# A hybrid encoder layer on one core: a third buffer for keys and values, and decays exponentiated a head ahead without the key norm

## The chip, the cores and the metric

The kernel runs on one core of one Trainium2 chip. The metric is device time in microseconds (us): the median over several executions, each timed on the device. Engines are named as the profile names them: PE (TensorE), DVE (VectorE), ACT (ScalarE), POOL (GpSimd), SP (SyncE).

## The reference

One encoder layer over 1024 tokens of width 1024, all in float32. After an RMSNorm one projection feeds two branches; only branch A (a gated delta rule in both directions, 8 heads of width 128) is touched by the change. Of it, per head and direction:

```python
    q = to_chunks(q * (dk ** -0.5))          # q, k l2-normalised per token
    g = jnp.cumsum(to_chunks(g), axis=-1)    # log decays
    diff = g[..., :, None] - g[..., None, :]
    decay = jnp.where(incl, jnp.exp(jnp.where(incl, diff, 0.0)), 0.0)
    kb = k * beta[..., None]
    lower = jnp.where(strict, jnp.einsum("bhnid,bhnjd->bhnij", kb, k) * decay, 0.0)
    rhs = jnp.concatenate([v * beta[..., None], kb * jnp.exp(g)[..., None]], axis=-1)
    sol = lax.linalg.triangular_solve(lower, rhs, left_side=True, lower=True,
                                      unit_diagonal=True)
    ...
    attn = jnp.einsum("bhnid,bhnjd->bhnij", q, k) * decay
    def step(S, inp):
        v_new = u_n - jnp.einsum("bhcd,bhde->bhce", w_n, S)
        o = (jnp.einsum("bhcd,bhde->bhce", qd_n, S)
             + jnp.einsum("bhij,bhje->bhie", attn_n, v_new))
        S = S * jnp.exp(gl_n)[..., None, None] + jnp.einsum("bhcd,bhce->bhde", kd_n, v_new)
```

q, k and v come from the projection through a centred convolution over 5 tokens and a SiLU. Branch B is a gated linear attention with 4 heads. Both are gated, projected, merged, projected once more and added to x.

## The kernel before

Tokens are cut into 8 chunks of 128 (NT), so a head has 16 units (U): 8 chunks in each direction. Branch A goes head by head, with four functions for each:

- `gdn_project(h)` multiplies the normalised input by the head's columns for q, k, v and z (four projections of 48 products of 128x128x512 each, tiles `pj_a` and `pj_z`), copies q, k and v into padded tiles `xp` and convolves them on VectorE by one multiplication (L516) and four multiply-adds (L518), in the order k, q, v. The SiLU (L499) of q, k, v and of the head before's z (`zs`) follows on ScalarE, between two loads of ScalarE's function tables: SiLU is in one table set, Exp and Ln in another.
- `gdn_decay(h)` fetches the head's cumulated log decays, spread over all partitions (1 MB, L580), into the tile `dt` and fills the half that must vanish with -1e30 by two selects on POOL (L585). There are two `dt` buffers; `dt` becomes the attention matrix later (L743) and is read to the end of the scan.
- `gdn_inverse(h)` builds the triangular inverse of all 16 units at once. The keys are transposed (`pk`), copied (`ktok`, L601) and squared with a sum (L605) into n2; rk2 = 1/n2. The Ln of n2 (L613) goes into a bias, and sixteen Exp (L622) make the decay times 1/n2 out of `dt`. Four products of VectorE (L633) multiply it with keys times keys (`pgr`) into `um`. Then come a small inverse of 32x32 blocks by 120 VectorE operations `tmp` and `yl` (L655, L657), products p, py, px, p2, p3 on TensorE that put blocks together, v times the key norm (L734) and `dt` times keys-queries (L743).
- `gdn_scan(h)` steps through the chunks in both directions: products `psc` (L781, L786, L796), r (L783), vd (L789), a copy vn on ScalarE (L791), the state S (L801), outputs `po` (L770); at its end o, osq and zs are combined and the head is written out.

What runs when is decided ahead of time: a scheduler lists the instructions of each engine in one fixed order, by the priorities that the blocks of the last loop set (a lower number goes first), by dependences and by free buffers. The inverse of head h+1 runs beside the scan of head h, and projections of the next heads, which have the last priority (P_FILL), fill TensorE in between; after head 7 thirteen gate projections (`pj_t`) do so, then branch B and the last projections follow. A tile asked for under a tag with n buffers waits until the tile n requests ago is no longer read: q, k and v (tags a0, a1, a2) have two buffers each, `xp` three. v's buffer is also `vtok`, which the scan reads to its end.

Of the kernel before, what the change touches and what calls it, by code (L numbers as in the profile page):

```python
# [8 lines left out]
F32 = mybir.dt.float32  # L9
F32R = mybir.dt.float32r  # L10
AF = mybir.ActivationFunctionType
ALU = mybir.AluOpType

P = 128
# [18 lines left out]

WRAW, WSPLIT, XS, XP = 2, 4, 4, 3

# [53 lines left out]
def layer_kernel(  # L89
# [43 lines left out]
    def by128(t):  # L133
        return t.rearrange("p (n i) -> p n i", i=P)
# [266 lines left out]
    def scan_gates(pool):  # L401
# [8 lines left out]
        smT = pool.tile([64, T], F32, tag="osq", name="smT", bufs=1)  # L410
        stl = pool.tile([P, 2, P], F32, tag="stl", name="stl", bufs=1)
        nc.scalar.dma_start(stl, consts[:, CONSTS["su"][0]:CONSTS["su"][0] + 2 * P].rearrange("p (d i) -> p d i", d=2))
        mid = pool.tile([P, 2, 130], F32, tag="t2", name="mid", bufs=4)
        nc.scalar.dma_start(mid, consts[:, o_c:o_c + 260].rearrange("p (d i) -> p d i", d=2))
        strict = [stl[:, d] for d in range(2)]
        ones = part(tb_, 3, 1)
# [30 lines left out]
        for d in range(2):  # L447
            rhs = lg[:, d].rearrange("p h n -> p (h n)")
            for q, m in enumerate((mask[d], strict[d], ones)):
                o = (d * 3 + q) * 64  # L450
                nc.tensor.matmul(psg[:, o:o + 64], lhsT=m, rhs=rhs, start=True, stop=True)

            o = 384 + d * 64
            nc.tensor.matmul(psg[:, o:o + 64], lhsT=mid[:, d, :P], rhs=rhs, start=True, stop=True)
        nc.scalar.activation(ev, psg[:, :384].rearrange("p (d q h n) -> p d q h n", d=2, q=3, h=HA), AF.Exp)
# [41 lines left out]
    def gdn_project(h, pool):  # L497
        a = [pool.tile([P, T], F32, tag=f"a{j}", name=f"{'qkv'[j]}{h}", bufs=2) for j in range(3)]
        silu = lambda t: tc.keep_in_program_order(nc.scalar.activation(t, t, AF.Silu))  # L499
# [76 lines left out]
    def gdn_decay(h, pool):  # L576


        dt = pool.tile([P, U, P], F32, tag="dt", name=f"dt{h}", bufs=2)
        nc.sync.dma_start(dt.rearrange("p u i -> p (u i)"),  # L580
                          cr_d[h:h + 1].rearrange("h d t -> h (d t)").broadcast_to([P, 2 * T]))
        for d in range(2):
            s = 1 - 2 * d
            us = slice(d * NT, (d + 1) * NT)
            nc.gpsimd.affine_select(dt[:, us], dt[:, us], pattern=[[0, NT], [s, P]], compare_op=ALU.is_ge,  # L585
                                    fill=-1e30, base=0, channel_multiplier=-s)
        return dt

    def gdn_inverse(h, pool, sm, qkv, dt):
# [21 lines left out]
        c2 = sm.tile([P, 2, NT], F32, tag="c2", name=f"c2_{h}")  # L611

        tc.keep_in_program_order(nc.scalar.activation(nk, n2, AF.Ln))  # L613
        bias = sm.tile([P, 2, NT], F32, tag="bias", name=f"bias_{h}")
        nc.vector.tensor_tensor(bias, nb[:, :, h], nk.unsqueeze(1).broadcast_to([P, 2, NT]), op=ALU.subtract)
        nc.vector.tensor_tensor(c1, be[:, :, h], rk2.unsqueeze(1).broadcast_to([P, 2, NT]), op=ALU.mult)
        nc.vector.tensor_tensor(c2, c1, ev[:, :, 1, h], op=ALU.mult)
        for g in range(2):
            for d in range(2):
                for n in range(4 * g, 4 * g + 4):  # L620
                    u = d * NT + n
                    nc.scalar.activation(dt[:, u], dt[:, u], AF.Exp, bias=bias[:, d, n:n + 1])  # L622


        um = pool.tile([P, U, P], F32, tag="um", name=f"um{h}", bufs=2)
        for g in range(2):
            pk = bank(pg, "g", f"pgr{h}_{g}")
            for j in range(4):
                ns = slice((4 * g + j) * P, (4 * g + j + 1) * P)
                nc.tensor.matmul(pk[:, j * P:(j + 1) * P], lhsT=kT[:, ns], rhs=kT[:, ns], start=True, stop=True)  # L630
            for d in range(2):
                us = slice(d * NT + 4 * g, d * NT + 4 * g + 4)
                nc.vector.tensor_tensor(um[:, us], by128(pk), dt[:, us], op=ALU.mult)  # L633

# [91 lines left out]

        tc.keep_in_program_order(nc.scalar.activation(nk, nk, AF.Exp, scale=0.5))

# [7 lines left out]
        for g in range(2):  # L736
# [4 lines left out]
            for d in range(2):  # L741
                us = slice(d * NT + 4 * g, d * NT + 4 * g + 4)
                nc.vector.tensor_tensor(dt[:, us], by128(pk), dt[:, us], op=ALU.mult)  # L743
        return dt, um, ktok, vtok, c2

    def gdn_scan(h, pool, sm, qkv, dt, um, ktok, vtok, c2):
        qT, kT, _ = qkv
# [24 lines left out]
        for s in range(NT):  # L772
# [12 lines left out]
            for d, n in un:  # L785
                nc.tensor.matmul(pc[d][:, P:2 * P], lhsT=um[:, d * NT + n], rhs=r[d], start=True, stop=True)  # L786
                if s < NT - 1:
                    vd[d] = sm.tile([P, P], F32, tag=f"vd{d}", name=f"vd{h}_{d}_{s}", bufs=1)
                    nc.vector.tensor_scalar(vd[d], pc[d][:, P:2 * P], c2[:, d, n:n + 1], None, op0=ALU.mult)  # L789
                vn[d] = sm.tile([P, P], F32, tag=f"vn{d}", name=f"vn{h}_{d}_{s}", bufs=1)  # L790
                nc.scalar.copy(vn[d], pc[d][:, P:2 * P])  # L791
            S0 = list(S)
# [363 lines left out]
```

## Time and profile before

| | |
|---|---|
| time, median of 3 runs | 1640.31 us (1637.06 to 1645.77) |
| the profiled execution | 1647.96 us, span of the trace 1646.2 us |
| TensorE busy | 1538.3 us, 93% |
| VectorE busy | 871.7 us, 53% |
| ScalarE busy | 704.3 us, 43% |
| GpSimd busy | 190.5 us, 12% |

The first two rows are device times; the profiled execution lies 7.65 us above the median and 1.76 us above its own span. Busy times are shares of the span. Branch A takes the first 870 us or so.

### The profile page before, as it was taken

What the parts mean: (1) busy time and instruction counts of PE and PEld (TensorE: products, weight loads), DVE (VectorE), ACT (ScalarE), POOL (GpSimd) and SP (SyncE); (2) the same over time, 40 slices, a digit from 0 to 9 for tenths busy, and PEclk for the clock granted to TensorE, in tenths of its full rate; (3) what the DMA queues carried; (4) which work ended last, traced back from release to release, by engine and by line L of the source; (5) the groups of instructions that cost most, each with busy time, mean ns of one, the idle gap of its engine ahead of it and who ended that gap; (6) DMA issues with size and microseconds to landing.
All of it is one profiled execution on the core that took longest, in us unless ns stands there. A gap on an engine that the chain in (4) does not pass through costs nothing.

```text
span 1646.2 us, 24982 instructions
## 1 busy us (share of the span) xinstructions
PE 1538.3 (93%) x9500; PEld 1295.8 (79%) x9500; DVE 871.7 (53%) x2252; ACT 704.3 (43%) x1488; POOL 190.5 (12%) x207
## 2 busy tenths in 40 slices
PE   6988978998998999899899999999999999999998
PEld 6867866777787878787677888898898988787887
DVE  5485485877879696878531012323314336445413
ACT  5452454436363635554332233535425545423311
POOL 3220111111213011110000020010120100000000
PEclk9996987999898999999999999999999999999999
DMA  5320221131212113131233322131131234755414
GB/s 160 126 68 18 80 71 33 33 106 36 96 46 90 46 33 116 50 99 48 77 121 100 103 65 64 27 103 33 55 85 48 80 100 143 238 157 173 128 45 154
DMA packets 142435, 142.07 MB, mean 86 GB/s; under 512 B 11419, under 2 KB 115403, under 8 KB 141285
## 3 DMA queue, kind: packets, MB, share of 16 engines
q1 hardware_dynamic: 134546, 126.11, 25.6%
q10 hardware_dynamic: 7128, 12.26, 2.4%
q0 software_dynamic: 640, 2.10, 0.4%
q8 instruction: 75, 1.23, 0.3%
q14 instruction: 46, 0.38, 0.1%
HBM read 109.98 MB, written 30.46 MB: 85 GB/s over the span
## 4 chain that ended last, share of the span: by engine, by line
PE 64%; DVE 16%; ACT 11%; DMA 5%; issue 3%; SPq 0%; POOL 0%; ACTq 0%; DVEq 0%; POOLq 0%
PE pj_t L252 8%; PE pj_y L252 7%; PE pj_v L241 6%; PE pout L141 5%; PE pj_g L252 5%; DVE yl L657 4%; PE pj_a L252 4%; DVE tmp L655 4%; PE pj_z L252 4%; PE pj_k L252 3%; PE pj_q L252 2%; ACT dt L622 2%; PE po L770 2%; PE psb L948 2%; PE pob L970 2%
## 5 line engine op out<-in xcount | busy, mean ns | idle before, releaser
L252 PE MATMUL pj_a<-hh,hi_a 128*128 128x512 f32 x368 | 153.6, 417 | 16.5 <-ACT xp L504 9.4
L252 PE MATMUL pj_a<-hl,hi_a 128*128 128x512 f32 x368 | 152.6, 415 | 0.0
L252 PE MATMUL pj_a<-hh,lo_a 128*128 128x512 f32 x368 | 152.1, 413 | 0.0
L252 PE MATMUL pj_t<-hh,hi_t 128*128 128x512 f32 x256 | 103.9, 406 | 2.8 <-ACT gt L282 2.8
L252 PE MATMUL pj_t<-hh,lo_t 128*128 128x512 f32 x256 | 104.2, 407 | 0.0
L252 PE MATMUL pj_t<-hl,hi_t 128*128 128x512 f32 x256 | 103.7, 405 | 0.0
L182 POOL TENSOR_TENSOR lo_a<-raw_a,hi_a 128x512 fp32r<-128x512 f32 x48 | 63.8, 1329 | 311.0 <-ACT hi_a L178 257.0
L252 PEld LDWEIGHTS pj_a<-hh,hi_a 128*128 128x128 f32 x368 | 73.0, 198 | 31.6 <-ACT xp L504 10.2
L657 DVE TENSOR_TENSOR yl<-yl,tmp 128x54 f32<-128x54 f32 (+13 forms) x480 | 96.3, 241 | 0.1
L655 DVE TENSOR_TENSOR tmp<-ulb,yl 128x54 f32<-128x54 f32 (+13 forms) x480 | 90.4, 228 | 0.1
L252 PEld LDWEIGHTS pj_a<-hl,hi_a 128*128 128x128 f32 x368 | 72.4, 197 | 13.9 <-issue 0.7
L252 PEld LDWEIGHTS pj_a<-hh,lo_a 128*128 128x128 f32 x368 | 72.4, 197 | 13.7 <-issue 0.8
L252 PE MATMUL pj_y<-ob,hi_y 128*128 128x512 f32 x256 | 79.1, 390 | 0.9 <-DVE gb L1075 0.9
L141 PE MATMUL pout<-wo,hh 128*128 128x512 f32 (+1 forms) x272 | 79.7, 377 | 0.0
L791 ACT COPY vn<-psc 128x128 f32<-128x128 f32 x128 | 32.2, 265 | 108.5 <-DVE vd L789 72.1
L241 PE MATMUL pj_v<-lo_v,hh 128*128 128x256 f32 x256 | 72.5, 283 | 0.0
L241 PE MATMUL pj_v<-hi_v,hl 128*128 128x256 f32 x256 | 72.5, 283 | 0.0
L241 PE MATMUL pj_v<-hi_v,hh 128*128 128x256 f32 x256 | 72.5, 283 | 0.0
L796 PE MATMUL psc<-vd,ktok 128*128 128x128 f32 x224 | 45.4, 304 | 24.8 <-ACT vn L791 24.7
L182 POOL TENSOR_TENSOR lo_v<-raw_v,hi_v 128x512 fp32r<-128x512 f32 x32 | 41.3, 1290 | 233.1 <-ACT hi_v L178 229.0
L796 PEld LDWEIGHTS psc<-vd,ktok 128*128 128x128 f32 x224 | 34.7, 198 | 39.5 <-ACT vn L791 37.7
L184 DVE TENSOR_TENSOR lo_t<-raw_t,hi_t 128x512 fp32r<-128x512 f32 x32 | 22.0, 689 | 71.7 <-ACT hi_t L178 71.7
(315 smaller groups left out, 4024.2 us busy)
## 6 DMA issues: line engine op xcount, KB each, us to landing
raw_a<-in_w_in_dram SPq DMA_DIRECT2D x48, 256.0 KB
dt<-cr_d SPq DMA_DIRECT2D x8, 1024.0 KB
qe<-eg_d SPq DMA_DIRECT2D x16, 512.0 KB
raw_t<-in_w_in_dram SPq DMA_DIRECT2D x32, 256.0 KB
gt_d<-gt SPq DMA_DIRECT2D x64, 128.0 KB
raw_v<-in_w_in_dram SPq DMA_DIRECT2D x32, 256.0 KB
xt<-in_x_dram SPq DMA_DIRECT2D x8, 512.0 KB
raw_z<-in_w_in_dram SPq DMA_DIRECT2D x16, 256.0 KB
```

The source lines that it names most:

```text
L141: nc.tensor.matmul(ps, lhsT=a(k), rhs=b(k), start=(s == 0), stop=(s == len(steps) - 1))
L182: nc.gpsimd.tensor_tensor(lo, raw, hi.bitcast(F32), op=ALU.subtract)
L241: nc.tensor.matmul(ps[b][:, c * 256:(c + 1) * 256], lhsT=a[th][:, kk, ts], rhs=w[:, k, :], start=kk == 0 and i == 0 and c == 0, stop=kk == ...
L252: nc.tensor.matmul(ps[:, cols], lhsT=a[:, k, :], rhs=b[th][:, kk, cols], start=kk == 0 and a is hi and b is src[0], stop=kk == KD - 1 and ...
L622: nc.scalar.activation(dt[:, u], dt[:, u], AF.Exp, bias=bias[:, d, n:n + 1])
L655: nc.vector.tensor_tensor(tv, ul2[:, i, 0:i].unsqueeze(2).broadcast_to([P, i, w_]), yv[:, i].unsqueeze(1).broadcast_to([P, i, w_]), op=ALU ...
L657: nc.vector.tensor_tensor(yv[:, 0:i], yv[:, 0:i], tv, op=ALU.subtract)
L770: nc.tensor.matmul(po_n(n), lhsT=lhsT, rhs=rhs, start=count[b] == 1, stop=count[b] == len(todo[b]))
L791: nc.scalar.copy(vn[d], pc[d][:, P:2 * P])
L796: nc.tensor.matmul(pc[d][:, 2 * P:3 * P], lhsT=ktok[:, ns], rhs=vd[d], start=True, stop=True)
L948: nc.tensor.matmul(p_s[:, :256], lhsT=ktok[:, u], rhs=vt[:, n], start=True, stop=True)
L970: nc.tensor.matmul(po[e][:, j * P:(j + 1) * P], lhsT=a, rhs=b, start=(i == 0), stop=(i == len(todo) - 1))
```

## The change

`A_BUFS` gives k (a1) and v (a2) three buffers, `xp` loses one, and two constant tiles share one buffer. `gdn_decay` exponentiates `dt` itself, with a bias that no longer holds the key norm. It is called for head h+1 right after the inverse of head h, so the sixteen Exp stand a head ahead of where their values are used. The factor 1/n2 comes back in two places: in `um`, by sixteen operations of 128x128 with rk2 as a scalar per partition, and in vn, by an ACTIVATE with rk2 as its scale. The Ln and Exp that make the key norm for v stand together behind p3.

```diff
-WRAW, WSPLIT, XS, XP = 2, 4, 4, 3
+WRAW, WSPLIT, XS, XP = 2, 4, 4, 2
+
+A_BUFS = (2, 3, 3)
...
-        stl = pool.tile([P, 2, P], F32, tag="stl", name="stl", bufs=1)
...
-        mid = pool.tile([P, 2, 130], F32, tag="t2", name="mid", bufs=4)
...
+        msk = pool.tile([P, 4, P], F32, tag="t2", name="msk", bufs=4)
...
-        a = [pool.tile([P, T], F32, tag=f"a{j}", name=f"{'qkv'[j]}{h}", bufs=2) for j in range(3)]
+        a = [pool.tile([P, T], F32, tag=f"a{j}", name=f"{'qkv'[j]}{h}", bufs=A_BUFS[j]) for j in range(3)]
...
             nc.gpsimd.affine_select(dt[:, us], dt[:, us], pattern=[[0, NT], [s, P]], compare_op=ALU.is_ge,
                                     fill=-1e30, base=0, channel_multiplier=-s)
+            for n in range(NT):
+                nc.scalar.activation(dt[:, d * NT + n], dt[:, d * NT + n], AF.Exp, bias=nb[:, d, h, n:n + 1])
         return dt
...
-
-        tc.keep_in_program_order(nc.scalar.activation(nk, n2, AF.Ln))
-        bias = sm.tile([P, 2, NT], F32, tag="bias", name=f"bias_{h}")
-        nc.vector.tensor_tensor(bias, nb[:, :, h], nk.unsqueeze(1).broadcast_to([P, 2, NT]), op=ALU.subtract)
...
-        for g in range(2):
-            for d in range(2):
-                for n in range(4 * g, 4 * g + 4):
-                    u = d * NT + n
-                    nc.scalar.activation(dt[:, u], dt[:, u], AF.Exp, bias=bias[:, d, n:n + 1])
...
-            for d in range(2):
-                us = slice(d * NT + 4 * g, d * NT + 4 * g + 4)
-                nc.vector.tensor_tensor(um[:, us], by128(pk), dt[:, us], op=ALU.mult)
+            for j in range(4):
+                n = 4 * g + j
+                for d in range(2):
+                    u = d * NT + n
+                    nc.vector.scalar_tensor_tensor(um[:, u], pk[:, j * P:(j + 1) * P], rk2[:, n:n + 1], dt[:, u],
+                                                   op0=ALU.mult, op1=ALU.mult)
...
-        tc.keep_in_program_order(nc.scalar.activation(nk, nk, AF.Exp, scale=0.5))
+        tc.keep_in_program_order(nc.scalar.activation(nk, n2, AF.Ln))
+        nc.scalar.activation(nk, nk, AF.Exp, scale=0.5)
...
-                nc.scalar.copy(vn[d], pc[d][:, P:2 * P])
+                nc.scalar.mul(vn[d], pc[d][:, P:2 * P], rk2[:, n:n + 1])
```

The scheduler lists every engine's instructions anew. Three places of these lists follow.

ScalarE, the front of head 4 (pk_1_4838 and pk_1_4893 are its keys in PSUM, the last squares; vn_0_3 and the like belong to scan 3, zs to head 3). Before:

```order
L605 ACTIVATE pk_1_4838,n_4_4827<-pk_1_4838 128x128
L791 COPY vn_0_3_4691<-psc_0_3_4680 128x128
L791 COPY vn_1_3_4696<-psc_1_3_4681 128x128
L613 ACT_TABLE_LOAD
L613 ACTIVATE nk_4849<-n_4_4827 128x8
L499 ACT_TABLE_LOAD
L499 ACTIVATE zs_4586<-zs_4586 128x1024
L622 ACT_TABLE_LOAD
L622 ACTIVATE dt_4285<-dt_4285,bias_4855 128x128 x16
L639 COPY ul_4890<-um_4875 32x32x8 x4
```

And in the changed kernel:

```order
L607 ACTIVATE pk_1_4893,n_4_4882<-pk_1_4893 128x128
L788 ACTIVATE vn_1_2_4723<-psc_1_2_4708,rk_3_3915 128x128
L788 ACTIVATE vn_0_3_4746<-psc_0_3_4735,rk_3_3915 128x128
L500 ACTIVATE zs_4641<-zs_4641 128x1024
L311 ACT_TABLE_LOAD
L180 CAST hi_a_5_0_5376<-raw_a_5_0_5374 128x512
L635 COPY ul_4938<-um_4911 32x32x8 x4
```

The Ln, the sixteen Exp and two of three table loads have left the stretch between the last squares and ul, the first copy out of um.

ScalarE behind the end of scan 2 (osq_3667 and osq_4655 belong to the ends of scan 2 and the start of scan 3, dt_4324 is head 4's dt, gz are head 4's z columns, q_4348 and q_4293 its q). Before:

```order
L727 ACTIVATE nk_3871<-nk_3871 128x8
L178 CAST hi_a_5_0_4546<-raw_a_5_0_4544 128x512
L282 COPY gz_0_0_4574<-pj_z_0_4512 128x256
L282 COPY gz_0_1_4577<-pj_z_0_4512 128x256
L791 COPY vn_0_0_4609<-psc_0_0_4604 128x128
L791 COPY vn_1_0_4614<-psc_1_0_4605 128x128
L178 CAST hi_a_5_1_5281<-raw_a_5_1_5279 128x512
...
L309 ACT_TABLE_LOAD
L499 ACTIVATE q_4293<-q_4293 128x1024
```

And in the changed kernel:

```order
L489 ACTIVATE osq_3667<-pm_a_1_3885,eps_eq 128x512
L490 ACTIVATE osq_3667<-osq_3667 128x1024
L788 ACTIVATE vn_0_0_4664<-psc_0_0_4659,rk_3_3915 128x128
L588 ACTIVATE dt_4324<-dt_4324,nb 128x128 x16
L752 ACTIVATE osq_4655<-q_3360 128x1024
L788 ACTIVATE vn_1_0_4669<-psc_1_0_4660,rk_3_3915 128x128
L284 COPY gz_0_0_4629<-pj_z_0_4567 128x256
L284 COPY gz_0_1_4632<-pj_z_0_4567 128x256
...
L311 ACT_TABLE_LOAD
L788 ACTIVATE vn_0_2_4718<-psc_0_2_4707,rk_3_3915 128x128
L500 ACTIVATE q_4348<-q_4348 128x1024
```

Head 4's sixteen Exp now stand between the first two vn of scan 3 and ahead of gz and of the SiLU of head 4.

VectorE, the convolution of head 3's keys (k3; numbers behind a name are heads: um2 and v2 belong to inversion 2, r1 and osq1 to scan 1). Before:

```order
L725 COPY um2_2919<-p3_2_3261 64x8x64
L801 SCALAR_TENSOR_TENSOR S1_1_6_2830<-S1_1_5_2802,ev_532,psc1_1_6_2809 128x128
L783 SCALAR_TENSOR_TENSOR r1_0_7_2839<-psc1_0_7_2836,nE_533,v1_1361 128x128
L734 TENSOR_TENSOR v2_2339<-pv2_0_3281,nk_2_2893 128x512
L734 TENSOR_TENSOR v2_2339<-pv2_1_3287,nk_2_2893 128x512
L783 SCALAR_TENSOR_TENSOR r1_1_7_2842<-psc1_1_7_2837,nE_533,v1_1361 128x128
L516 TENSOR_SCALAR k3_3316<-xp1_3_3318,cw_110 128x1024
L743 TENSOR_TENSOR dt2_2329<-pkq2_0_3293,dt2_2329 128x512 x2
L743 TENSOR_TENSOR dt2_2329<-pkq2_1_3300,dt2_2329 128x512 x2
L817 TENSOR_TENSOR osq1_2644<-osq1_2644,o1_2854 128x512 x2
L518 SCALAR_TENSOR_TENSOR k3_3316<-xp1_3_3318,cw_110,k3_3316 128x1024
```

And in the changed kernel:

```order
L702 COPY um1_1947<-py_1_2226 32x8x32 x2
L703 COPY xa1_2185<-px_1_2259 32x8x32
...
L517 TENSOR_SCALAR k3_3361<-xp1_3_3363,cw_110 128x1024
L519 SCALAR_TENSOR_TENSOR k3_3361<-xp1_3_3363,cw_110,k3_3361 128x1024
L721 COPY um1_1947<-p3_1_2301 64x8x64
...
L731 TENSOR_TENSOR v1_1386<-pv1_0_2322,nk_1_1940 128x512
...
L740 TENSOR_TENSOR dt1_1360<-pkq1_0_2334,dt1_1360 128x512 x2
```

The convolution moved from the end of scan 1 and of inversion 2 to the end of inversion 1, a head earlier. On TensorE the transposes of head 3's keys (pk) stood 95 rows behind the last products of inversion 2 (pkq) and stand 2 rows behind them now.

## Rows read from the trace of the kernel before

**Rows 1.** the page, part 1: busy us, share of the span, instructions

```profile
PE 1538.3 (93%) x9500; PEld 1295.8 (79%) x9500; DVE 871.7 (53%) x2252; ACT 704.3 (43%) x1488; POOL 190.5 (12%) x207
```

**Rows 2.** busy time of each engine in stretches of the span

```profile
core 0: us, PE busy (x) PEld busy (x) DVE busy (x) ACT busy (x) POOL busy (x), PEclk, DMA share, GB/s
...
471.00:560.00 89.00, 82.34 (x593) 68.10 (x592) 69.92 (x211) 43.80 (x98) 19.15 (x18) 0.92 0.22 69
...
870.00:1000.00 130.00, 129.36 (x664) 110.80 (x664) 17.50 (x26) 36.02 (x76) 13.51 (x12) 1.00 0.32 87
sum 915.00, PE 834.74 PEld 697.03 DVE 583.38 ACT 398.72 POOL 123.14; mean PE 92.75 PEld 77.45 DVE 64.82 ACT 44.30 POOL 13.68
```

**Rows 3.** the chain of waits, parts of it in order: start, us, what

```profile
260.93 3.03 PE p L686 x64
...
330.34 1.84 PE p L686 x64
...
377.97 2.25 ACT pk L605 x16
...
432.63 2.52 PE p L686 x64
...
849.58 8.22 PE pj_t L252 x36
```

**Rows 4.** ScalarE in order of time, front of head 4

```profile
473.30 1.28 ACT L613 ACT_TABLE_LOAD   x1
...
474.82 1.28 ACT L499 ACT_TABLE_LOAD   x1
476.11 1.06 ACT L499 ACTIVATE zs<-zs 128x1024 f32<-128x1024 f32 x1
477.18 1.28 ACT L622 ACT_TABLE_LOAD   x1
478.47 4.80 ACT L622 ACTIVATE dt<-dt,bias 128x128 f32<-128x128 f32 x16
```

**Rows 5.** VectorE in order of time, fronts of heads 2 and 4

```profile
290.01 0.17 DVE L608 TENSOR_SCALAR n<-n 128x8 f32<-128x8 f32 x1 [0.95 <-ACT pk L605]
...
295.57 0.69 DVE L633 TENSOR_TENSOR um<-pgr,dt 128x512 f32<-128x512 f32 x1 [0.48 <-ACT dt L622]
...
472.99 0.17 DVE L608 TENSOR_SCALAR n<-n 128x8 f32<-128x8 f32 x1 [0.72 <-ACT pk L605]
...
473.64 0.17 DVE L617 TENSOR_TENSOR c<-c,ev 128x16 f32<-128x16 f32 x1
...
483.30 0.69 DVE L633 TENSOR_TENSOR um<-pgr,dt 128x512 f32<-128x512 f32 x1 [0.48 <-ACT dt L622]
```

**Rows 6.** groups by line: busy us, mean ns, idle before and what ended it

```profile
L622 ACT ACTIVATE dt<-dt,bias 128x128 f32<-128x128 f32 x128 | 38.3, 388 | 0.4 <-DVE bias L615 0.3
L791 ACT COPY vn<-psc 128x128 f32<-128x128 f32 x128 | 32.2, 265 | 108.5 <-DVE vd L789 72.1 <-PE psc L786 17.8 <-DVE tmp L655 12.5
...
L518 DVE SCALAR_TENSOR_TENSOR k<-xp,cw,k 128x1024 f32<-128x1024 f32 x32 | 43.4, 1357 | 0.1
...
L783 DVE SCALAR_TENSOR_TENSOR r<-psc,nE,v 128x128 f32<-128x128 f32 x112 | 36.9, 344 | 13.2 <-PE psc L781 11.2
...
L633 DVE TENSOR_TENSOR um<-pgr,dt 128x512 f32<-128x512 f32 x32 | 22.1, 691 | 27.7 <-ACT dt L622 24.5 <-PE pj_z L252 3.1
```

**Rows 7.** waits of the weight load queue, 284 to 870 us: total, times, longest

```profile
PEld psc L796 <- ACT vn L791: 35.6, 32, 3.8
```

**Rows 8.** fetches and selects of dt, SP and POOL in order of time

```profile
418.80 0.46 SPq L580 DMA_DIRECT2D dt<-cr_d  x1
...
424.69 3.92 POOL L585 TENSOR_SCALAR_AFFINE_SELECT dt<-dt 128x1024 f32<-128x1024 f32 x2 [6.38 <-DMA dt<-cr_d]
...
514.54 0.34 SPq L580 DMA_DIRECT2D dt<-cr_d  x1
...
519.16 5.81 POOL L585 TENSOR_SCALAR_AFFINE_SELECT dt<-dt 128x1024 f32<-128x1024 f32 x2
```

More of the change, by code (lines that the diff above doesn't have):

```diff
@@ L410, in scan_gates @@
         smT = pool.tile([64, T], F32, tag="osq", name="smT", bufs=1)
-        stl = pool.tile([P, 2, P], F32, tag="stl", name="stl", bufs=1)
-        nc.scalar.dma_start(stl, consts[:, CONSTS["su"][0]:CONSTS["su"][0] + 2 * P].rearrange("p (d i) -> p d i", d=2))
-        mid = pool.tile([P, 2, 130], F32, tag="t2", name="mid", bufs=4)
-        nc.scalar.dma_start(mid, consts[:, o_c:o_c + 260].rearrange("p (d i) -> p d i", d=2))
-        strict = [stl[:, d] for d in range(2)]
+        msk = pool.tile([P, 4, P], F32, tag="t2", name="msk", bufs=4)
+        nc.scalar.dma_start(msk[:, 0:2], consts[:, CONSTS["su"][0]:CONSTS["su"][0] + 2 * P].rearrange("p (d i) -> p d i", d=2))
+        nc.scalar.dma_start(msk[:, 2:4], consts[:, o_c:o_c + 260].rearrange("p (d i) -> p d i", d=2)[:, :, :P])
+        strict, mid = ([msk[:, 2 * q + d] for d in range(2)] for q in range(2))
         ones = part(tb_, 3, 1)
@@ L453, in scan_gates @@
             o = 384 + d * 64
-            nc.tensor.matmul(psg[:, o:o + 64], lhsT=mid[:, d, :P], rhs=rhs, start=True, stop=True)
+            nc.tensor.matmul(psg[:, o:o + 64], lhsT=mid[d], rhs=rhs, start=True, stop=True)
         nc.scalar.activation(ev, psg[:, :384].rearrange("p (d q h n) -> p d q h n", d=2, q=3, h=HA), AF.Exp)
@@ L743, in gdn_inverse, with gdn_scan @@
                 nc.vector.tensor_tensor(dt[:, us], by128(pk), dt[:, us], op=ALU.mult)
-        return dt, um, ktok, vtok, c2
-    def gdn_scan(h, pool, sm, qkv, dt, um, ktok, vtok, c2):
+        return dt, um, ktok, vtok, rk2, c2
+    def gdn_scan(h, pool, sm, qkv, dt, um, ktok, vtok, rk2, c2):
         qT, kT, _ = qkv
```

## The prediction

> **What bounds the kernel now.** I read the busy times first. TensorE is busy 93% of the span, VectorE 53%, ScalarE 43% [rows 1]. The table by stage then shows where TensorE is not full: between 85 and 1000 us it is idle for 915.00 - 834.74 = 80.3 us, and from 870 us on, when the gate projections fill it, it is busy 129.36 of 130 us [rows 2]. So whatever the change gives must come out of the eight heads of branch A: the number of products is the same before and after, and the end is their time plus TensorE's idle and slow stretches.
>
> Next I read the chain of waits by its marks, one per head: the first products p of a head's inversion (line 686) [rows 3]. From one mark to the next I cut three parts: the **middle** (p of head h to the last square of head h+1's keys), the **front** (those squares to the last um), and the **inversion** (um to p, almost all of it VectorE, 120 small tmp/yl operations and what the scheduler put between them). Head 4's front stands as it ran on ScalarE [rows 4] and VectorE [rows 5]: a table load for the Ln, a load and the SiLU of zs, another load, then sixteen Exp in 4.80 us; VectorE's four um products wait for them one by one. From 472.99 to 483.30 + 0.69 it is 11.0 us; heads 3 to 7 are all alike. Head 2 has no loads there and takes 290.01 to 296.26, 6.3 us [rows 5]. Head 1, read in the same way, lies at 10.2.
>
> **The change, part by part.**
>
> *The front.* The Ln, the bias and the Exps are gone. What is left is n2, rk2, c1 and c2 (472.99 to 473.64 + 0.17: 0.82 us) [rows 5] and sixteen um operations of 128x128 where there were four of 128x512. No such um is in the trace. The nearest row is r (line 783): the same operation, one PSUM operand, a scalar per partition, 128x128, 344 ns by its mean [rows 6]; two behind each other overlap by some 0.05, and I take 0.30 each: 4.8 us, bounds 0.27 and 0.344, that is 4.3 to 5.5. The new front is 0.8 + 4.8 = 5.6 us. Saved: 5.4 us in each of heads 3 to 7 (4.7 to 5.9 by the bounds), 4.6 in head 1, 0.7 in head 2. Head 0 loses: the Exps of dt(0) and dt(1) come into ScalarE's order ahead of what its front needs; I count twelve Exps of 0.30 us start to start (4.80 / 16 [rows 4]) that nothing hides, +3.4 net of the two loads that go. Sum of the fronts: -27.0 - 4.6 - 0.7 + 3.4 = -28.9 us.
>
> [...]
>
> The split therefore costs VectorE about 4.8 - 2.8 = 2.0 us a head by rows, which is inside the 5.4 above.
>
> *The loads.* In the orders ScalarE has 57 table loads before and 42 after. Each takes 1.28 us, and the next ACTIVATE starts 0.01 us behind it (477.18 + 1.28, then 478.47) [rows 4]: 15 x 1.28 = 19 us of ScalarE, nearly all off the path once the front's are counted above, since ScalarE is idle over half of each head [rows 2].
>
> [...]
>
> *The inversion.* The third buffers let convolution passes start earlier, and the scheduler puts them between the tmp/yl operations, on the path. By the two orders, with 1.2 us for a pass of 1024 elements (1.36 by its mean, which overlaps the next), 0.69 for one of 512 and 0.34 for a scan operation [rows 6]: head 6 gets 9 more passes, 2 more of 512 and 13 fewer scan operations, 10.8 + 1.4 - 4.4 = +7.8. Heads 1 to 5 in the same way +1.4, +2.7, -2.1, -0.6, +3.4; head 7 nothing. Sum +12 us (0 if scan operations leaving a head were as dear to it as passes coming in, 15 with 1.36).
>
> *The middles.* Head 2's is where the third k buffer acts. Before, k(3)'s convolution waits for the end of scan(1), and the middle lasts from 330.34 to 377.97 + 2.25, 49.9 us [rows 3]; after, it stands before the end of inversion 1, and pk(3) comes two rows behind pkq(2) in TensorE's order. Head 1's middle, where nothing waits, is 260.93 to 290.01, 29.1 us [rows 3, 5]. Between -20.8 and 0 I take -11, since five more table loads and the Exps of dt(3) stand there now. Head 3's is where the early Exps stand in the way. dt has two buffers, so dt(4) is fetched only when scan(2) has ended: issued at 418.80, landed for the selects at 424.69, 3.92 us of selects [rows 8], then 4.8 of Exp: 5.9 + 3.9 + 4.8 = 14.6 us. Before, the Exps stood far behind; now vn_1_0, gz and head 4's SiLU are queued behind them on ScalarE, and TensorE's next scan step and projection banks wait for these. About half can hide behind products already under way: +8 (0 to 14.6). For the others I went by the work in the two orders (products of 512 columns at 8.22 / 36 = 0.23 us [rows 3], passes at 1.2): head 0 +4.9 (the Exps of dt(2) ahead of gz and SiLU), head 1 -3.6 (loads and zs leave), head 4 +5 and head 5 +3 (more projection and scan products fall into them), head 6 -4.4. Sum: -11 + 8 + 4.9 - 3.6 + 5 + 3 - 4.4 = +2 us (-15 to +15).
>
> *vn.* The copy becomes an ACTIVATE with a scalar per partition. The nearest row with one is the Exp, 388 ns, against 265 for the copy [rows 6]: +0.12 us. TensorE's next scan product does wait for vn (35.6 us in 32 waits [rows 7]). 64 steps on the path would be 7.7 us; the wait is named as vn's, though it often ends with the vd or psc before it, so I take +1.5 (0 to 7.7).
>
> *The tail* after head 7's p is mostly dense and has the same products; fewer loads there: -2 (-4 to 0). Buffers, the merged mask tile and two instead of three xp buffers add no instruction on the path; an xp that comes free late shows up as a later convolution, which the middles hold.
>
> **Sum.** -28.9 + 12 + 2 + 1.5 - 2 = -15.4 us. The profiled execution took 1647.96 us, 7.65 above the median of 1640.31; I subtract from the median: 1625 us.
>
> **Rivals.**
>
> *The fronts come through whole.* The extra passes lie where VectorE would have waited (it is idle 19 of 89 us even in a head [rows 2]), and the Exps of dt find their data landed. For it: VectorE's waits inside inversions; against it: the inversion is a chain of short operations with almost no gap. Without the +12 and the +8: -35.4, about 1605 us.
>
> *The bound is TensorE.* In head 4 it is busy 82.34 of 89 us [rows 2]: 6.7 us of slack, and the front was filled with projection products, back to back. If shorter fronts only push those products into the middles, the gain stops where the slack does: heads 1 and 6, whose work by the orders fills 66 to 69 us of the 68 that I leave them, give nothing back, and heads 3 to 5 about half: some -5 to -8, about 1634 us.
>
> *Slower: the Exps block ScalarE.* What I count once, in head 3, happens in every head from 3 to 6: ScalarE's queue stands at the first Exp until scan(h-1) has ended, dt has landed and POOL has run its selects (up to 5.81 us for dt(5), issued at 514.54, selected from 519.16 [rows 8]). By 10.5 to 15.3 us a head, less what hides, +10 in three further heads: 1625 + 30 = 1655 us. It decides from the point where the landing comes more than some 5 us after the turn of the SiLU: then each head loses what its front gained. For it: two dt buffers only, and vn in the same queue; against it: in heads 4 to 6 the fetches before the change were issued while ScalarE had other work.
>
> **How the numbers follow.** My forecast 0.40, fronts whole 0.18, TensorE bound 0.22, slower 0.20. Half a per cent of 1640 is 8.2 us, about what a measurement of this kernel can tell from no change. Faster (below 1632): 0.40 + 0.18 = 0.58; same 0.22 (the TensorE case, whose 1634 lies there); slower 0.20. The likeliest case alone reaches from 1615 to 1632. To leave out 2 in 10 the range goes down to the whole fronts with the low um price, 1602, and up into the first part of the slower case, 1648.
>
> **What would show it.** In the profile after: um's sixteen operations at about 0.30 us, and squares to last um at 5.6 us in heads 3 to 7; no table load there. k(3)'s passes before the end of inversion 1, and 11 us less between p(2) and head 3's squares. A gap on ScalarE before dt(4)'s Exps, 10 us or more behind scan(2)'s end. Head 6's inversion 8 us longer. vn at 0.39 us. I am wrong if the inversions of heads 5 and 6 take much more or less than reckoned, if the gap before the Exps stands in several heads, or if TensorE's idle time in the heads does not fall by about 15 us.

## The result: faster by 1.1%

The changed kernel takes 1626.05 us (median of 4 runs, 1622.71 to 1628.17) against 1643.04 us for the kernel before (4 runs): ratio 0.9894, 95% interval 0.9856 to 0.9931. Run once more beside other kernels it came to 0.9899 (0.9852 to 0.9946). The forecast was 1625, and the change is faster by more than the half per cent at which the prediction drew the line. Part of the close agreement is luck: the prediction took 15.4 us off a median of 1640.31, and beside the changed kernel the kernel before came to 1643.04, so the measured gain is 17.0 us (by the interval 11 to 24).

### The profile page after: what moved, and what is told of

Read it like the earlier page. It is cut to its first block, busy times and chain, and to the rows that moved or that the text cites. A ratio compares the mean times of both kernels' runs of the same rounds, so it can differ in the third digit from the quotient of the medians.

```text
span 1624.2 us, 25070 instructions
## 1 busy us (share of the span) xinstructions
PE 1531.2 (94%) x9500; PEld 1290.5 (79%) x9500; DVE 881.9 (54%) x2340; ACT 696.9 (43%) x1473; POOL 193.8 (12%) x207
## 4 chain that ended last, share of the span: by engine, by line
PE 67%; DVE 16%; ACT 7%; DMA 6%; issue 2%; SPq 2%; POOL 1%; DVEq 0%; ACTq 0%; POOLq 0%
PE pj_t L254 9%; PE pj_y L254 8%; PE pj_v L243 6%; PE pout L143 5%; PE pj_a L254 5%; PE pj_g L254 5%; DVE tmp L651 4%; DVE yl L653 4%; PE pj_k L254 3%; PE pj_z L254 3%; PE pj_q L254 2%; PE po L767 2%; PE psb L945 2%; PE pob L967 2%; PE psc L793 2%
## 5 line engine op out<-in xcount | busy, mean ns | idle before, releaser
L184 POOL TENSOR_TENSOR lo_a<-raw_a,hi_a 128x512 fp32r<-128x512 f32 x48 | 70.0, 1457 | 281.3 <-ACT hi_a L180 259.1
L788 ACT ACTIVATE vn<-psc,rk 128x128 f32<-128x128 f32 x128 | 45.2, 366 | 120.8 <-DVE vd L786 73.5
L653 DVE TENSOR_TENSOR yl<-yl,tmp 128x54 f32<-128x54 f32 (+13 forms) x480 | 90.9, 231 | 0.1
L180 ACT CAST hi_a<-raw_a 128x512 fp32r<-128x512 f32 x48 | 29.7, 620 | 67.0 <-PE pj_a L254 38.0
L143 PEld LDWEIGHTS pout<-wo,hh 128*128 128x128 f32 x272 | 50.1, 188 | 9.5
L793 PE MATMUL psc<-vd,ktok 128*128 128x128 f32 x224 | 47.2, 305 | 11.0 <-ACT vn L788 11.0
```

The costliest lines, as they stand in the source:

```text
L143: nc.tensor.matmul(ps, lhsT=a(k), rhs=b(k), start=(s == 0), stop=(s == len(steps) - 1))
L180: i = nc.scalar.copy(hi, raw)
L184: nc.gpsimd.tensor_tensor(lo, raw, hi.bitcast(F32), op=ALU.subtract)
L653: nc.vector.tensor_tensor(yv[:, 0:i], yv[:, 0:i], tv, op=ALU.subtract)
L788: nc.scalar.mul(vn[d], pc[d][:, P:2 * P], rk2[:, n:n + 1])
L793: nc.tensor.matmul(pc[d][:, 2 * P:3 * P], lhsT=ktok[:, ns], rhs=vd[d], start=True, stop=True)
```

## The profile after

First the page of the changed kernel, busy time by engine (it answers to [rows 1]), and the last line of its table by stage, 85 to 1000 us (to [rows 2]):

```profile
PE 1531.2 (94%) x9500; PEld 1290.5 (79%) x9500; DVE 881.9 (54%) x2340; ACT 696.9 (43%) x1473; POOL 193.8 (12%) x207
```

```profile
sum 915.00, PE 850.54 PEld 710.82 DVE 593.88 ACT 393.57 POOL 129.50; mean PE 94.50 PEld 78.98 DVE 65.99 ACT 43.73 POOL 14.39
```

The count of products is the same. In the stretch TensorE is idle for 915.00 - 850.54 = 64.5 us, where it was 80.3: 15.8 us less.

The chain of waits gives the first products p of the inversions again (start, us, what; heads 1 to 4, 6 and 7):

```profile
260.87 3.06 PE p L682 x64
...
339.28 1.84 PE p L682 x64
...
424.22 1.89 PE p L682 x64
...
515.93 1.91 PE p L682 x64
...
700.76 2.59 PE p L682 x64
...
766.23 1.84 PE p L682 x64
```

With the same cuts as before the prediction, from the two profiled executions (spans 1646.2 and 1624.2 us):

| part, us | before | after | difference | predicted |
|---|---|---|---|---|
| head 0 up to the last um | 99.9 | 100.9 | +1.0 | +3.4 |
| fronts of heads 1 to 7 | 72.3 | 39.3 | -33.0 | -32.3 |
| inversions, 8 heads | 306.2 | 320.6 | +14.4 | +12 |
| middles, 7 | 305.5 | 305.4 | -0.1 | +2 (vn's +1.5 beside it) |
| from head 7's p to the end | 862.2 | 858.0 | -4.2 | -2 |

The parts add up to 22 us, more than the 17.0 between the medians: the profiled execution of the kernel before took 5 us more than its median, that of the changed kernel 1 us more. By the two pages 14.9 of the 22 us are idle time of TensorE (its span less its busy time, 107.9 and 93.0 us), and 7.1 are a shorter busy time for the same 9500 products.

So the fronts gave 33 us, and the inversions took 14 of it back. The front of head 4 shows the gain. VectorE in order of time, then ScalarE (start, us, line, operation; they answer to [rows 4, 5]):

```profile
471.22 0.17 DVE L610 TENSOR_SCALAR n<-n 128x8 f32<-128x8 f32 x1 [1.68 <-ACT pk L607]
...
471.87 0.18 DVE L615 TENSOR_TENSOR c<-c,ev 128x16 f32<-128x16 f32 x1
472.21 4.23 DVE L628 SCALAR_TENSOR_TENSOR um<-pgr,rk,dt 128x128 f32<-128x128 f32 x16 [0.16 <-PE pgr L623]
```

```profile
471.59 1.05 ACT L500 ACTIVATE zs<-zs 128x1024 f32<-128x1024 f32 x1
472.66 1.28 ACT L311 ACT_TABLE_LOAD   x1
```

The sixteen um operations follow c2 after 0.16 us and need 4.23 us, 0.26 each; ScalarE's one load runs beside them. The front is 5.2 us, where it was 11.0.

And the loss. VectorE's groups in head 6's inversion alone, before (666.9 to 706.9 us) and after (651.6 to 700.8), columns as in [rows 6]:

```profile
L518 DVE SCALAR_TENSOR_TENSOR k<-xp,cw,k 128x1024 f32<-128x1024 f32 x3 | 3.8, 1279 | 0.0
L518 DVE SCALAR_TENSOR_TENSOR q<-xp,cw,q 128x1024 f32<-128x1024 f32 x2 | 2.6, 1278 | 0.0
```

```profile
L651 DVE TENSOR_TENSOR tmp<-ulb,yl 128x60 f32<-128x60 f32 (+34 forms) x60 | 12.9, 254 | 1.0 <-DMA yl<-in_consts_dram 1.0
...
L519 DVE SCALAR_TENSOR_TENSOR q<-xp,cw,q 128x1024 f32<-128x1024 f32 x4 | 5.1, 1278 | 0.0
L519 DVE SCALAR_TENSOR_TENSOR k<-xp,cw,k 128x1024 f32<-128x1024 f32 x4 | 5.1, 1275 | 0.0
L519 DVE SCALAR_TENSOR_TENSOR v<-xp,cw,v 128x1024 f32<-128x1024 f32 x3 | 3.8, 1255 | 0.0
```

Eleven multiply-adds of a convolution where there were five. This inversion takes 49.1 us, where it took 40.1.

## Experiments

For each kernel I cut the same parts and counted, in VectorE's order, the work that stands inside the inversions of heads 1 to 7. The count takes 1.2 us for a convolution pass, 1.15 to 1.4 for another of 1024 elements, 0.65 for one of 512, 0.3 for a scan operation, and some 6 us a head for the inversion's own copies. Times are medians; ratios are to runs of the kernel before on the same chip.

### The two halves apart

Buffers alone, on the kernel before:

```diff
-WRAW, WSPLIT, XS, XP = 2, 4, 4, 3
+WRAW, WSPLIT, XS, XP = 2, 4, 4, 2
+A_BUFS = (2, 3, 3)
```

> The kernel before with the third k and v buffers, two xp buffers and the merged mask tile, and nothing of the new decay. By my sum: head 2's middle about 14 us shorter, but by its order VectorE has 15 us more of passes inside the inversions, fronts as before: within 6 us of the kernel before, about 1643. By the rival that the buffers carry the gain: about 1628. By the rival that they only crowd VectorE: about 1658.

1632.1 us, ratio 0.9926 (0.9887 to 0.9964). In the profiled execution inversions were 17.2 us longer and middles 12.8 shorter, so the sums came out near the 15 and 14 expected. But the 14 were to lie in head 2's middle, and that lost only 3.3 us (46.5); head 3's lost 15.4 and head 4's gained 13.7. Third buffers by themselves do not shorten head 2's middle: here VectorE's work in it still holds four multiply-adds of q and the last of k. With fronts (-4.1) and tail (-4.3) the span was 4.2 us shorter. The median shows more, 11 us, which is nearer the rival's 1628 than my 1643. The granted clock of these runs was 0.967 (median) against 0.959 for the kernel before beside them, and such a step goes with about that much time (14.6 us for 0.01 on this chip, last section); whether the clock is the cause or follows from the order is open.

Decay alone, on the changed kernel:

```diff
-WRAW, WSPLIT, XS, XP = 2, 4, 4, 2
-A_BUFS = (2, 3, 3)
+WRAW, WSPLIT, XS, XP = 2, 4, 4, 3
+A_BUFS = (2, 2, 2)
```

> The changed kernel with two buffers for k and v and three for xp, as before; the new decay alone. By my sum: fronts 32 us shorter, inversions 10 us shorter by the order (fewer passes between), head 2's middle as in the kernel before, the early Exps +8 to +15 in the middles: 1609 to 1618, that is faster than the changed kernel. By the rival that the buffers carry the gain: about 1640. By the rival that both parts are needed (the head-ahead Exps stall without early keys): slower than the changed kernel's 1626.

1614.9 us, ratio 0.9811 (0.9775 to 0.9847): in time as the sum said, and 11 us below the changed kernel. Fronts (-32.4 against the kernel before) and inversions (-12.3) came as expected; the middles cost 22.4, more than the 8 to 15, and the tail gave back 10.8 that the sum did not hold. It was run once more beside the changed kernel:

> The changed kernel once more, beside the decay alone on the same chip. Ratio to the kernel before 0.989 as first measured (0.986 to 0.993).

> The decay alone (two buffers for k and v, three for xp) once more. If the third k and v buffers in place of the third xp buffer really cost the changed kernel time, it is again some 11 us faster than the changed kernel beside it (ratio to before about 0.981). If the first difference came from the two chips, both are alike within 4 us.

1625.8 us (0.9899, 0.9852 to 0.9946) and 1614.4 us (0.9840, 0.9794 to 0.9885). The medians differ by 11 us a second time, though these two intervals overlap. The parts say where: against the changed kernel, the decay alone has inversions 26.7 us shorter (293.9), middles 22.4 us longer (327.8; head 2's is 49.6 again) and a tail 6.6 us shorter. In this pair the buffers mostly move convolution passes from the middles into the inversions. The two halves do not add: the buffers alone gained 11 us on the kernel before, and cost 11 us on top of the new decay.

### Which buffer

```diff
-A_BUFS = (2, 3, 3)
+A_BUFS = (2, 2, 2)
```

> The new decay with two buffers for q, k, v and two for xp: it tells the third xp buffer of the decay-alone kernel apart from the k and v buffers. Foreign VectorE work inside the inversions of heads 1 to 7 by its order: 133 us, against 128 with three xp buffers and 149 in the changed kernel. By the rule that such work lengthens the inversions (1.5 us for 1 us of it over the kernels so far): 7 us slower than the decay alone, about 1620. By the rival that xp buffers do nothing: about 1614.

1643.3 us, ratio 0.9996 (0.9969 to 1.0024). All of the decay's gain is gone with one xp buffer fewer. Both guesses were far off. Inversions took 270.1 us in heads 1 to 7, as counted (267.9), 8.6 more than in the decay alone; the tail is 12 us longer. One wait goes with two xp buffers. TensorE's waits that end with xp, then ScalarE's xp copies, in this kernel between 85 and 870 us:

```profile
PE pj_z L254 <- ACT xp L505: 5.2, 2, 4.6
PE pj_a L254 <- ACT xp L505: 1.6, 1, 1.6
```

```profile
L505 ACT COPY xp<-pj_a 128x512 f32<-128x512 f32 x42 | 24.1, 585 | 31.7 <-PE pj_a L254 22.9 <-DVE k L519 7.9 <-DVE q L519 0.8
```

A copy waits 7.9 us for k's convolution to leave its xp buffer, and the z projection waits behind it; in the decay-alone kernel, with three xp buffers, no copy waits for VectorE:

```profile
L505 ACT COPY xp<-pj_a 128x512 f32<-128x512 f32 x42 | 24.3, 585 | 29.0 <-PE pj_a L254 28.9
```

That is not what sets this kernel apart, though: the changed kernel, which also has two xp buffers, shows the copies waiting for k's convolution too (3.5 us, and 7.1 when it was run once more), and it is 17 us faster. TensorE is idle 75.1 us between 85 and 1000 us here and 61.8 in the decay alone. Those 13 us are most of the 19 by which the two profiled executions differ; the medians differ by 28. The runs also had a lower clock (0.957 against 0.968 in the mean), which by the slopes of the last section goes with about the rest; why this order has it is not settled.

```diff
-WRAW, WSPLIT, XS, XP = 2, 4, 4, 2
-A_BUFS = (2, 3, 3)
+WRAW, WSPLIT, XS, XP = 2, 4, 4, 3
+A_BUFS = (2, 2, 3)
```

> The new decay with a third buffer for v alone, three xp. Foreign work inside the inversions 136 us by its order, nearly all of the extra in head 6: by the rule the inversions take 11 us more than in the decay-alone kernel, and middles give some of it back: 1616 to 1624. By the rival that it is the third k buffer that costs in the changed kernel and v's is free: about 1613.

1621.5 us, ratio 0.9868 (0.9830 to 0.9906). Inversions of heads 1 to 7: 272.6 us, as the count said to the tenth and 11 more than in the decay alone; by them v's third buffer is not free. The time lies 7 us above the decay alone, with intervals that overlap.

And with `A_BUFS = (2, 3, 2)` in the same place:

> The new decay with a third buffer for k alone and three for xp. Foreign VectorE work inside the inversions of heads 1 to 7 by its order 143 us, so by the line through the kernels so far (9.5 us a head and 1.52 us for 1 us of such work) these inversions take 283 us, against 261 in the decay alone. Head 2's middle 14 us shorter as in the changed kernel. Together some 5 to 10 us slower than the decay alone, about 1622. By the rival that early keys pay and passes in the inversion don't matter: faster than the decay alone by 10.

1635.0 us, ratio 0.9944 (0.9911 to 0.9978), 13 us above what I expected. Inversions 279.5 us (counted 283), head 2's middle 34.1 us as hoped; but head 3's front took 15.1 us. ScalarE in order of time, then VectorE:

```profile
384.06 1.06 ACT L500 ACTIVATE v<-v 128x1024 f32<-128x1024 f32 x1
385.14 1.28 ACT L588 ACT_TABLE_LOAD   x1
386.43 4.79 ACT L588 ACTIVATE dt<-dt,nb 128x128 f32<-128x128 f32 x16
```

```profile
378.52 1.28 DVE L519 SCALAR_TENSOR_TENSOR v<-xp,cw,v 128x1024 f32<-128x1024 f32 x1
...
382.99 2.13 DVE L127 TENSOR_TENSOR zs<-osq,zs 128x1024 f32<-128x1024 f32 x1
...
387.78 0.34 DVE L628 SCALAR_TENSOR_TENSOR um<-pgr,rk,dt 128x128 f32<-128x128 f32 x1
```

The squares are done at 378.3 us. Two things stand in this front. dt(3), which needs scan(1)'s dt buffer, is fetched at 374.4, selected until 382.8 and exponentiated only by 391.2, behind v's SiLU and a table load, so the last um could not come earlier. And VectorE's order has two passes of v, zs, qe and o before the first um; it works on them almost without a gap until 387.8, and then um follows at once. So even here neither ScalarE nor VectorE stands still for dt; that dt's lateness made the scheduler put this work there is likely, not shown. Head 6's middle of 47.5 us was not in my sum either. The rival, that early keys pay, is out for this order.

### Running a head ahead

Exps tied back to their own head:

```diff
-            for n in range(NT):
-                nc.scalar.activation(dt[:, d * NT + n], dt[:, d * NT + n], AF.Exp, bias=nb[:, d, h, n:n + 1])
...
+        bias = sm.tile([P, 2, NT], F32, tag="bias", name=f"bias_{h}")
+        nc.vector.scalar_tensor_tensor(bias, n2.unsqueeze(1).broadcast_to([P, 2, NT]), 0.0, nb[:, :, h],
+                                       op0=ALU.mult, op1=ALU.add)
+        for g in range(2):
+            for n in range(4 * g, 4 * g + 4):
+                for d in range(2):
+                    u = d * NT + n
+                    nc.scalar.activation(dt[:, u], dt[:, u], AF.Exp, bias=bias[:, d, n:n + 1])
```

> The changed kernel with the sixteen Exps tied back to their own head's front (the bias is nb plus zero times n2, so they can't start before the squares), still without the key norm in them. By my sum: each front 2.4 us longer than in the changed kernel (7.7 us, one load more behind it), +17 us, against no early Exps in the middles, -10, and 5 us fewer passes inside the inversions: about 1628, the same as the changed kernel. By the rival that running a head ahead is what pays: the whole 4.8 us of Exps in eight fronts and nothing back, about 1660.

1651.8 us, ratio 1.0045 (1.0014 to 1.0075). My expectation failed. The fronts of heads 1 to 7 were 17.0 us longer than in the changed kernel, as expected (8.1 us in most); head 0's was 5.8 longer, but its squares ended 6.6 earlier. What failed is the rest: the middles got only 4.5 shorter, not 10, the inversions 3.8 longer, not 5 shorter, and the tail 9.7 longer, with a granted clock of 0.86 against 0.93 in the first 100 us behind head 7's p. So running ahead is worth the 17 us of the fronts, of which the middles take 4.5; the other 13 or so of the 26 us come with the new order and the clock and are not shown to be the Exps'.

Exps behind the scan's work, on the decay alone:

```diff
-            for n in range(NT):
-                nc.scalar.activation(dt[:, d * NT + n], dt[:, d * NT + n], AF.Exp, bias=nb[:, d, h, n:n + 1])
+        with at(P_HEAD * h + P_Z + 1000):
+            for d in range(2):
+                for n in range(NT):
+                    nc.scalar.activation(dt[:, d * NT + n], dt[:, d * NT + n], AF.Exp, bias=nb[:, d, h, n:n + 1])
```

> The decay alone, with the Exps of dt(h) at a priority behind the scan of the head before, so that vn of that scan goes first on ScalarE where both are ready. Foreign work inside the inversions 128 us by its order, the same as in the decay alone: inversions about 262 us. If the early Exps in ScalarE's queue hold the middles up (my +8), it is 4 to 8 us faster than the decay alone; if they don't, since ScalarE waits for dt only 1.1 us in all in the changed kernel, the same within 4 us.

1608.7 us, ratio 0.9803 (0.9751 to 0.9854), against 0.9840 for the decay alone beside it. The intervals overlap, so the 6 us are not certain. By the trace the tail is 5 us shorter than in both executions of the decay alone, and so is head 0's inversion. Head 0's last um ends at 96.5 us instead of 102.7 (its squares end 10 us earlier, ahead of Exps that stood before them), while the middles are 329.3 us against 335.1 and 327.8 in two executions of the decay alone. So the early Exps are not shown to hold the middles up. Inversions 264.0 us (counted 260.5).

A third dt buffer:

```diff
-A_BUFS = (2, 3, 3)
+A_BUFS = (2, 2, 2)
...
-        dt = pool.tile([P, U, P], F32, tag="dt", name=f"dt{h}", bufs=2)
+        dt = pool.tile([P, U, P], F32, tag="dt", name=f"dt{h}", bufs=3)
```

> The changed kernel with three dt buffers in place of the third k and v buffers (xp two), so that dt(h+1) is fetched, selected and exponentiated a scan earlier. By my sum: no Exp waits for a scan's end, -7 in head 3's middle and -5 in head 1's; inversions 19 us shorter by the order; head 2's middle +14 without the third k buffer: about 1610. By the rival that dt's arrival limits nothing: no faster than the decay alone with two buffers.

1619.8 us, ratio 0.9840 (0.9804 to 0.9877), 10 us above my sum; 5 us above the decay alone, 23 below the same buffers with two for dt. Inversions are 24.5 us shorter than in the changed kernel (19 expected), but the middles 27.8 longer, where the sum had 2. Its head-3 middle is 42.1 us (46.9 in the changed kernel), so there -4.8 of the 7 expected, but head 6's is 48.6. As three dt buffers change the order everywhere, this does not price dt's arrival by itself.

### vn and um

```diff
-                nc.scalar.mul(vn[d], pc[d][:, P:2 * P], rk2[:, n:n + 1])
+                nc.scalar.copy(vn[d], pc[d][:, P:2 * P])
```

> The changed kernel with vn as the plain copy of before; 1/n2 is left out of vn. Up to head 4's inversion VectorE's order has the same work, so that stretch prices vn: by my term 0.5 to 1 us shorter up to there (1.5 over all heads), by its upper bound of 0.10 us on every step 3 us. Behind it the order differs, with 6.5 us less foreign work inside the inversions: by the rule 10 us, so about 1615 over all; by vn alone 1624.

1623.9 us, ratio 0.9872 (0.9826 to 0.9918). At the last square of head 4 it was 7.9 us ahead of the changed kernel, of which 6.5 lie in head 1's middle, where the changed kernel's clock stands at 0.50 from 260 to 280 us: the 6.5 may be the clock's, so no price for vn can be read from that. The weight load queue's waits for it between 284 and 870 us can: 18.0 us in 29 with the copy, 20.9 in 34 with the scalar. So vn costs some 0 to 3 us by an estimate from these sums, whose waits stand in different orders. The 10 us counted for the inversions did not come (3.2 shorter), so that the time fits "by vn alone" shows little.

```diff
-            for j in range(4):
-                n = 4 * g + j
-                for d in range(2):
-                    u = d * NT + n
-                    nc.vector.scalar_tensor_tensor(um[:, u], pk[:, j * P:(j + 1) * P], rk2[:, n:n + 1], dt[:, u],
-                                                   op0=ALU.mult, op1=ALU.mult)
+            for d in range(2):
+                us = slice(d * NT + 4 * g, d * NT + 4 * g + 4)
+                nc.vector.scalar_tensor_tensor(um[:, us], by128(pk), 0.01, dt[:, us], op0=ALU.mult, op1=ALU.mult)
```

> The changed kernel with um in four operations of 128x512 with the constant 0.01 in place of sixteen with rk2; 1/n2 is left out of um, 0.01 stands for it. By my sum: fronts 1.7 us shorter in each head (5.3 to 3.6), -13; inversions by the order 4 us less foreign work, -6: about 1608. By the rival that fronts are hidden behind TensorE's products by now: 1620 or more.

1633.6 us, ratio 0.9928 (0.9900 to 0.9956): above the changed kernel and 26 us above my sum. The rival's "1620 or more" holds the time, but not by what it said, for the fronts did shorten, by 15.9 us (3.6 in most), and the inversions by 10; but the middles grew by 42.6, in heads 2 and 6 above all (59.5 and 47.2 us, 36.1 and 29.0 in the changed kernel). The scheduler had laid out everything anew. The gain of the part was real and was lost in places that the edit does not touch. Head 2's middle is long here with three k buffers.

### The count of work inside the inversions

Over heads 1 to 7 of the first six kernels (before, changed, buffers, decay, own head, three dt) the length of an inversion follows the count with a correlation of 0.96: 9.5 us + 1.52 times the count. This line, fixed then, gave the later six sums of seven inversions as 267.9, 272.6, 282.5, 286.3, 282.9 and 260.5 us; measured were 270.1, 272.6, 285.1, 282.6, 279.5 and 264.0. It is a correlation over schedules, not a test that moved single passes, and why 1 us counted costs 1.5 is open (scan operations may wait for TensorE there).

## Why the prediction was right, point by point

**Fronts.** Right: 5.2 to 5.4 us in most heads. The operation has 342 ns by its mean, about as r had (344); in a row they take 0.26 each, just under the lower bound of 0.27. The overlap of 0.05 that I gave r was too small: its rows in the trace before show 0.08 (20 pairs, 0.27 us start to start). Groups of the changed kernel by line:

```profile
L628 DVE SCALAR_TENSOR_TENSOR um<-pgr,rk,dt 128x128 f32<-128x128 f32 x128 | 34.0, 342 | 1.6 <-PE pgr L623 1.4
...
L788 ACT ACTIVATE vn<-psc,rk 128x128 f32<-128x128 f32 x128 | 45.2, 366 | 120.8 <-DVE vd L786 73.5 <-PE psc L783 20.2 <-DVE tmp L651 14.1
...
L588 ACT ACTIVATE dt<-dt,nb 128x128 f32<-128x128 f32 x128 | 38.8, 388 | 1.3 <-POOL dt L585 1.1
```

Head 0 lost 1.0, not 3.4: its squares end 7.0 us later, and its front is 6.0 shorter. Head 3's front is 6.9 us from its last square; n starts 1.1 us behind that there.

**Inversions.** +14.4 against +12 (the six terms add up to 12.6); head 6 +9.1 against +7.8, of which 1.0 is a wait for the fetch of yl that I had not seen. Heads 1 to 5 took +3.0, +4.3, +0.6, -3.3 and +2.4 (+1.4, +2.7, -2.1, -0.6 and +3.4). In head 3 another wait stands that the count could not hold. The last um ends at 382.2 us, but the copies ul out of um stand behind zs's SiLU on ScalarE, and that waits for the fetch of zs, which has one buffer; from the chain of waits:

```profile
376.91 5.95 DMA zs<-z_d
...
384.22 1.06 ACT zs L500
385.28 0.54 ACT ul L635
```

**Middles.** The sum is right, the parts less so; that their errors cancel is luck. Heads 0, 4, 5 and 6 took +0.8, +1.9, +2.9 and -3.7 (+4.9, +5, +3 and -4.4). Head 2's: -13.7 against -11. With the new decay as it is, this goes with k's third buffer: 36.1 us here and 34.1 with k's alone, 49.6 without and 47.5 with v's alone. The buffer is needed for it but not enough, for with it the buffers-alone kernel has 46.5 and the one with four um operations 59.5; the scheduler also has to use it for k(3). More was to be had: dt(3)'s Exps still stand among head 3's squares, on the chain of waits:

```profile
364.77 0.37 ACT pk L607 x2
365.20 0.31 issue
365.51 0.67 ACT pk L607 x4
366.18 0.58 ACT osq L489
366.77 1.28 ACT L588
368.07 4.79 ACT dt L588 x16
```

Head 3's: +6.7 against +8, but not by the mechanism I gave. ScalarE waits for dt only 1.1 us in the whole kernel (last row of the groups above). The chain there is VectorE's:

```profile
445.22 1.99 DVE osq L814 x2
447.21 1.21 DVE v L519
448.44 1.28 DVE v L519
449.72 0.26 DVE vd L786
450.00 0.35 DVE vd L786
450.35 1.40 DVE v L519
451.75 2.03 DVE zs L127
453.78 1.14 DVE qe L749
454.91 1.32 DVE o L476 x2
```

Scan 2 ends at 444 us now, behind head 3's p at 424.2; its closing operations (osq, zs, qe and o, 6.5 us of these rows) fall into this middle, where before the scan had ended at 418, ahead of p at 432.6, and they lay inside the inversion. The passes of v stood in this middle before too. The work that left head 3's inversion in my count came back here. So in the changed kernel nothing is left of the slower rival: dt's queue does not block. In the run with k's third buffer alone dt comes late in one head, but ScalarE does not stand still for it there either.

Head 1's middle is the wrong term: +5.1 against -3.6. I had reckoned it by the work alone, at full clock. The loads did go, but TensorE's clock stayed low longer. Table by stage, 250 to 290 us, before and then after (stretch, its length, busy time and count of PE, PEld, DVE, ACT, POOL; the number behind POOL's count is the granted clock):

```profile
250.00:260.00 10.00, 3.51 (x16) 2.58 (x14) 9.94 (x20) 0.36 (x1) 1.97 (x4) 0.80 0.20 52
260.00:270.00 10.00, 9.07 (x164) 8.22 (x165) 3.25 (x10) 4.35 (x12) 0.00 (x0) 0.50 0.09 28
270.00:280.00 10.00, 10.00 (x87) 8.04 (x88) 1.42 (x3) 6.90 (x11) 1.26 (x1) 0.85 0.19 55
280.00:290.00 10.00, 10.00 (x69) 8.73 (x68) 4.93 (x10) 9.48 (x26) 1.78 (x2) 1.00 0.15 46
```

```profile
250.00:260.00 10.00, 2.30 (x11) 1.56 (x9) 9.79 (x29) 3.96 (x5) 1.30 (x5) 0.72 0.10 26
260.00:270.00 10.00, 9.13 (x164) 8.26 (x165) 3.42 (x10) 4.33 (x11) 1.08 (x1) 0.50 0.11 28
270.00:280.00 10.00, 10.00 (x66) 8.00 (x66) 2.94 (x4) 2.01 (x4) 1.26 (x1) 0.50 0.01 2
280.00:290.00 10.00, 10.00 (x56) 8.70 (x56) 7.13 (x10) 1.00 (x3) 0.00 (x0) 0.75 0.10 26
```

That is (0.85 - 0.50) x 10 + (1.00 - 0.75) x 10 = 6.0 us of full-speed work missing, most of the 8.7 us by which the term was off. The second execution of the changed kernel has the same (0.50 and 0.77), so this belongs to its order; what in the order does it is open.

**vn.** Waits of the weight load queue for it, 284 to 870 us (35.6 us in 32 before [rows 7]):

```profile
PEld psc L793 <- ACT vn L788: 20.9, 34, 2.8
```

An ACTIVATE is 0.10 us longer (366 ns against the copy's 265), and the waits named after it are shorter. That fits what was predicted, that vn is rarely what the product really waits for, but the order changed as well.

**The rivals.** Whole fronts without a price inside the inversions: out, the price was 14 us. The bound by TensorE: out at this size, since its idle time fell by 15.8 us, as the sum wanted. What I had priced at nothing, two xp buffers in place of three, was inside the orders from which I counted, so the sum held it; the experiments show, twice, that the exchange of buffers keeps the changed kernel some 11 us above its better half. Within the exchange the parts do not add: with the new decay, going from three xp buffers to two costs 28 us, and third buffers for k and v on top of that win 17 back, while with three xp buffers either third buffer made the median higher, k's clear of the intervals. Third buffers for both beside three for xp were not run.

## What to carry to other kernels

Time taken out of a chain is kept only if the scheduler doesn't put other work into it or move work elsewhere: count what stands between the chain's operations in the new order, before and after, and price it. An extra buffer was paid for with another here, and the price was higher than the gain; try the half of a change that needs no buffer by itself. Exponentials that need no late input can run ahead at little cost: tying them back made the fronts 17 us longer, and the middles only 4.5 shorter. An edit that wins in its own place can lose more elsewhere, as the four um operations did, so price a part from the trace and not only from the total.

## What the runs showed of the hardware

Executions of one kernel differ by some 20 us, and the time goes with TensorE's clock: over 23 executions of the kernel before on one chip (1634 to 1653 us) the time falls by 13.9 us for each 0.01 of mean granted clock, with a correlation of -0.93; over 19 and 17 on other chips by 14.6 and 14.8. That is about what the clock itself would give, by an estimate: 0.01 of 0.96 on 1538 us of busy TensorE is 16 us. In the rows above the clock is at 0.80 and 0.72 in the 10 us in which TensorE is busy for 3.51 and 2.30 us, waiting for the end of an inversion. Behind it TensorE is busy again, 9.07 and 9.13 of the next 10 us and then all of them, yet the clock is at 0.50 for 10 us in the kernel before and for 20 us in the changed one. Two executions of the changed kernel are nearly alike there (0.75 and 0.77 from 280 to 290 us). By these rows, which are of one head, a wait for an inversion would cost a second time after it has ended, and medians of two kernels could differ by several us through this alone (6.0 us by the estimate for head 1's middle); that is an estimate too, and no run here tested it by itself.
